# Turning tiles by VectorE blocks and a round trip through DRAM, in one layer of a hybrid decoder

## The chip, the cores and the metric

The kernel runs on one core of a Trainium2 chip. The metric is device time in microseconds. Five engines work side by side, each through its own instructions in order: TensorE (PE in the profile, with PEld for its weight loads), VectorE (DVE), ScalarE (ACT), GpSimd (POOL) and SyncE (SP), which here issues nearly all DMAs.

## The reference

One layer, with 512 prompt tokens (rows) and 8 decode tokens with a past of 1024 keys. All is fp32.

```python
h = einsum('btd,de->bte', x, w_in)             # 1024 -> 256+256+512+16+512 + 4 x 512
qa, ka, va, za, ga, qb, kb, vb, gb = split(h)
# A: gated linear attention, 4 heads, decay from za, state S_t = diag(a_t) S_(t-1) + k_t^T v_t
new_state = exp(b_last)[..., None] * state + einsum('bhsd,bhsv->bhdv', kc * exp(b_last - b), vc)
# B: attention, 8 heads, windows (128,1), (512,4), (2048,16), bias by distance from a table
o_b = prompt_dilated(qb, kb, vb, rel_bias)
mix = concat([o_a * silu(ga), o_b * silu(gb)])
y = einsum('bte,ed->btd', mix, w_out)
x_new = layer_norm(DEEPNORM_ALPHA * x + y, ln_g, ln_b)
```

Outputs are x_new, the new states of A, and the key and value rows of B, for prompt and decode tokens.

## The kernel before

**Products.** An fp32 product is made of three matmuls of parts: the high part of one side by the high part of the other, high by low, and low by high. So every weight tile is loaded (`raw_*`), rounded on ScalarE (`hi_*`), and its rest taken on VectorE (`lo_*`).

**Layouts.** Rows 256 to 511 of the values (va of A, vb of B) and of the output y come out with tokens on partitions, by matmuls of 256 columns (`ps_va_2`, `ps_y`). For rows 0 to 255 the weights stand still in TensorE and 264 columns stream past, 256 prompt rows and the 8 decode tokens. That gives features on partitions (`ps_va_f`, `ps_vb_f`, `ps_yf`), so those tiles have to be turned before they can be used with tokens on partitions. A tile of 128 features (`f`) by 256 tokens is turned by two TensorE transposes of 128x128; two such tiles make a group of 256 columns (`i` or `g`).

- Values: `turn` copies the products to SBUF (`feat`), frees their PSUM bank, and turns into another (`ps_turn`); `va_into` and `vb_into` copy that into `va0` or `v{i}`.
- Decayed keys of A: `gla_state` turns `kd` into `kt` (`ps_kt`), eight transposes and two copies; TensorE then forms the states (`ps_kv`) from `kt` and the values.
- Output: `out_turn` copies to `feat_y`, turns into `ps_yt`, and starts two `out_evac`, which add the result to ALPHA times x in the row tiles `y`, straight from PSUM, with the statistics (`bn_stats`) behind each addition.

**Attention bias.** `bias_table` writes a table `tab` of one row per head to DRAM and copies each row 35 times (`tabr`); `strips` reads, per head and half, a 128-row strip in which each partition is shifted against the one above, with two DMAs for the second half.

**The order of the work.** All is written as generators that yield instructions, marks to wait for (`At`) and buffers to wait for (`Need`, from the slots in `SLOTS`). `add(task, priority)` hands one to `Plan`, which estimates when each waiting instruction could start, by costs in `Op`, and emits the one that starts first; the priority decides between equals. Hence all instructions have line 377 in the profile, and are told apart by their tiles. `dense` with priority 100 is the stream of projections (its sequence is `ORDER`), into which the rest is woven. `LATE` is the planner's allowance for a DMA behind others, and a DMA also waits for the one eight before it (`RING`).

**The end.** `out_first` makes the output of rows 0 to 255, then `out_unit` that of rows 256 to 511 (`ps_y`). The last 256 columns of the last row tile are added up in PSUM on top of x, by `seed` and `last_norm`; the 256 before them go through `early_mean`. The other row tiles are normalized by `norm` as their four statistics are there: a centring with `gamma` and a scaling with `rstd` and `beta`, each a VectorE pass of 128x1024.

Of the kernel before, what the change touches and what calls it, by code (L numbers as in the profile page):

```python
# [20 lines left out]
P = 128  # L21
DM = 1024
KT = DM // P
NP = 512
# [33 lines left out]
T_R = 35  # L58
# [6 lines left out]
SLOTS = dict(  # L65
    g=23,
    w=8, r=3,
    sv=4,
    pt=2, far=5, tp=2, vp=2,
    t2=2, st=3,  # L70
    pr=4,
    t1=5, ob=3,
    m=6)
# [5 lines left out]
LATE = 1000.0  # L79
# [5 lines left out]
ORDER = "qa0 qb0 qb1 qb2 qb3 kb0 kb1 vb0 kb2 kb3 gb0 vb1 gb1 gb2 va0 gb3 va1 ga0 ga1 ga2 ga3".split()  # L85


class Op:
# [3 lines left out]
    def __init__(self, eng, fn, args, kw):  # L92
# [13 lines left out]
        if fn == "dma_start":  # L106
# [4 lines left out]
            rate = 130 if run <= 128 else 175 if x.ap[0][1] <= 64 else 340 if run >= 4096 else 230  # L111
            self.xfer = max(4 * total(x) / rate, 200)
            self.late = 600 * (rate == 175)
# [12 lines left out]
        elif eng.name == "DVE":  # L126
            fast = fn in ("tensor_copy", "tensor_scalar", "memset") and not psum
            ptr = fn in ("tensor_scalar", "scalar_tensor_tensor") and any(size(x) == 1 for x in aps[1:]) and n > 1
            c = ((n / 2 if fast else n) + (155 if fn == "transpose" else 124 if ptr else 66)) / .96
# [7 lines left out]
def run_of(x):  # L137

    n = 1
    for step, c in reversed(x.ap[1:]):  # L140
        if step != n:
            break
        n *= c
    return n

# [236 lines left out]
def trunk(ctx: ExitStack, tc: tile.TileContext, xT, xp, xs, state, ck, cv, w_in, wab, gnorm,  # L382
# [23 lines left out]
    def rsqrt(o, x, scale, eps, between=None):  # L406
# [4 lines left out]
        if between:  # L411
# [3 lines left out]
            add(between, 5)  # L415
# [365 lines left out]
    def dense():  # L781
# [28 lines left out]
        add(gate_decay(pz), 24.7)  # L810
# [66 lines left out]
    def bias_table():  # L877
        yield At("const")
        tab = dram.tile([HB, T_P], F32, name="tab")
# [111 lines left out]
    def gla_state():  # L991
# [120 lines left out]
    def parts(n, own, m, scale):  # L1112

        def evac(ps, u):
# [870 lines left out]
```

## Time and profile before

| | |
|---|---|
| time, 3 runs | 275.93, 277.95, 278.9 us; median 277.95 |
| span of the profiled execution (first to last instruction) | 275.6 us |
| the profiled execution's own time | its span; the nearest timed run, 275.93, is 0.3 above it |
| TensorE busy | 266.9 us (97%) |
| VectorE, ScalarE, GpSimd busy | 214.6, 158.5, 52.8 us |
| DMA | 52.58 MB in 61527 packets, mean 191 GB/s |
| granted TensorE clock | 0.996 |

The span in 40 slices, the busy share in tenths:

```profile
PE   8999999999899999999999999999999999999990
DVE  4845899998989497998396963738999999239984
ACT  4727886475538583877686824535668886224401
DMA  7977939436967898556497979893897660980432
```

A group row gives engine, operation, tile written <- tiles read, shape and count, then the busy time in us and the mean of one in ns, then the idle time ahead of it and who ended it. In a timeline a row is start, duration, engine, line, instruction, and in brackets the wait just before it. A row of the chain is start, length, engine, tile, and how many instructions it joins; its lengths do not overlap.

### The profile page before, as it was taken

Reading aid. Unit: us, or ns where it says so; the run is one execution under the profiler, and the core shown is the slowest. Engines: PE = TensorE matmul, PEld = TensorE weight load, DVE = VectorE, ACT = ScalarE, POOL = GpSimd, SP = SyncE. Lnnn points to the kernel's source line nnn. Section 1 sums busy time; section 2 is a strip of 40 time slices with the busy share of each in tenths; the row PEclk is TensorE's granted clock in tenths of the full one; section 3 lists DMA queues with packets and bytes.
Section 4 is the critical chain, followed back from the end, with each engine's and each line's share of the span. In section 5 each row is a group of like instructions: output and inputs, shape, how many; then the busy total and the mean of one; then the engine's idle time right before and its main releaser. Section 6 shows DMA issues by size and latency. Waiting matters only on the chain.

```text
span 275.6 us, 7460 instructions
## 1 busy us (share of the span) xinstructions
PE 266.9 (97%) x2881; PEld 252.1 (91%) x2881; DVE 214.6 (78%) x578; ACT 158.5 (58%) x478; POOL 52.8 (19%) x71
## 2 busy tenths in 40 slices
PE   8999999999899999999999999999999999999990
PEld 5999999999899989989999999999999999998890
DVE  4845899998989497998396963738999999239984
ACT  4727886475538583877686824535668886224401
POOL 3000000000534260703000633744242000000000
PEclk9999999999999999999999999999999999999998
DMA  7977939436967898556497979893897660980432
GB/s 219 340 181 190 266 91 235 125 104 179 311 188 161 243 291 276 157 115 157 87 258 195 221 202 188 250 279 92 265 246 194 179 223 6 293 239 0 180 129 76
DMA packets 61527, 52.58 MB, mean 191 GB/s; under 512 B 13645, under 2 KB 53715, under 8 KB 61493
## 3 DMA queue, kind: packets, MB, share of 16 engines
q1 hardware_dynamic: 60917, 51.66, 67.2%
q8 instruction: 22, 0.36, 0.5%
q10 hardware_dynamic: 576, 0.46, 0.5%
q14 instruction: 12, 0.10, 0.1%
HBM read 46.02 MB, written 6.42 MB: 190 GB/s over the span
## 4 chain that ended last, share of the span: by engine, by line
PE 94%; DVE 4%; ACT 1%; issue 0%; DVEq 0%
PE ps_ga L377 9%; PE ps_gb L377 9%; PE ps_qb L377 9%; PE ps_yf L377 8%; PE ps_kb L377 8%; PE ps_y L377 7%; PE ps_qa L377 5%; PE ps_ka L377 4%; PE ps_vb_f L377 4%; PE ps_va_f L377 4%; PE ps_vb L377 4%; PE ps_va L377 4%; PE ps_pv L377 3%; PE ps_s L377 3%; PE ps_pt L377 2%; PE ps_oa L377 2%
## 5 line engine op out<-in xcount | busy, mean ns | idle before, releaser
L377 POOL TENSOR_TENSOR past<-past,qbc 128x256 f32<-128x256 f32 x32 | 24.0, 782 | 99.5 <-DMA qbc<-qsd 91.6
L377 POOL TENSOR_TENSOR vv<-vv,pb 128x256 f32<-128x256 f32 x32 | 26.5, 860 | 55.3 <-DMA pb<-psd_s 49.4
L377 ACT ACTIVATE pr<-pr,ms 128x128 f32<-128x128 f32 (+3 forms) x48 | 22.8, 493 | 6.7 <-DVE ms L377 6.5
L377 DVE CUSTOM_DVE_ANT_0 pr<-ps_s,strip 128x128 f32<-128x128 f32 (+3 forms) x32 | 11.8, 410 | 6.9 <-PE ps_s L377 6.0
L377 ACT COPY pt<-ps_pt 128x256 f32<-128x256 f32 (+1 forms) x27 | 9.3, 354 | 11.1 <-PE ps_pt L377 11.1
L377 ACT ACTIVATE sg<-sg 128x264 f32<-128x264 f32 (+1 forms) x32 | 13.4, 420 | 0.5
L377 PE MATMUL ps_ka<-xx,hi_ka 128*128 128x264 f32 (+1 forms) x64 | 12.8, 296 | 0.0
L377 PE MATMUL ps_pt<-cf,pr 128*128 128x128 f32 x56 | 11.0, 274 | 0.0
L377 PEld LDWEIGHTS ps_ka<-xx,hi_ka 128*128 128x128 f32 x64 | 10.4, 201 | 0.0
L377 DVE TENSOR_REDUCE lt<-past 128x8 f32<-128x512 f32 x16 | 10.4, 671 | 0.0
L377 ACT ACTIVATE d<-d 128x512 f32<-128x512 f32 x11 | 6.9, 648 | 5.8 <-DVE d L377 5.8
L377 DVE TENSOR_REDUCE o_pv<-vv 128x4 f32<-128x1024 f32 x8 | 9.7, 1210 | 0.0
L377 ACT COPY feat_y<-ps_yf 128x256 f32<-128x256 f32 x7 | 2.6, 373 | 11.2 <-PE ps_yf L377 11.2
L377 PE MATMUL ps_ka<-xx,lo_ka 128*128 128x264 f32 (+1 forms) x32 | 9.0, 293 | 0.0
L377 DVE SCALAR_TENSOR_TENSOR y<-y,ps_yt 128x256 f32<-128x256 f32 x8 | 3.0, 418 | 6.9 <-PE ps_yt L377 6.9
L377 DVE SCALAR_TENSOR_TENSOR s<-v,ka_s,s 128x128 f32<-128x128 f32 x16 | 5.1, 343 | 3.2 <-DMA v<-vad 1.9
L377 PE MATMUL ps_qa<-xx,hi_ka 128*128 128x264 f32 (+1 forms) x32 | 7.4, 310 | 0.0
L377 PEld LDWEIGHTS ps_pt<-cf,pr 128*128 128x128 f32 x56 | 6.9, 140 | 0.3 <-issue 0.2
L377 PE MATMUL ps_kb<-xx,hi_kb__744 128*128 128x264 f32 (+1 forms) x32 | 6.2, 293 | 0.9 <-DVE ms L377 0.9
L377 PE MATMUL ps_pv<-pt,v 128*64 128x128 f32 (+1 forms) x80 | 6.9, 318 | 0.0
L377 PE MATMUL ps_gb<-xx,hi_gb__1903 128*128 128x264 f32 (+1 forms) x32 | 6.8, 295 | 0.0
L377 ACT CAST xx<-x_raw 128x520 fp32r<-128x520 f32 (+2 forms) x10 | 5.3, 539 | 2.6 <-DMA x_raw<-in_xT_dram 2.3
(570 smaller groups left out, 1065.8 us busy)
## 6 DMA issues: line engine op xcount, KB each, us to landing
past<-in_ck_dram SPq DMA_DIRECT2D x8, 512.0 KB
vv<-in_cv_dram SPq DMA_DIRECT2D x8, 512.0 KB
pb<-psd_s SPq DMA_DIRECT2D x16, 256.0 KB
s<-in_state_dram SPq DMA_DIRECT2D x4, 512.0 KB
strip<-tabr SPq DMA_DIRECT2D x16, 128.0 KB
qbc<-qsd SPq DMA_DIRECT2D x8, 256.0 KB
y<-in_xp_dram SPq DMA_DIRECT2D x4, 512.0 KB
x_raw<-in_xT_dram SPq DMA_DIRECT2D x6, 260.0 KB
```

The costliest lines, as they stand in the source:

```text
L377: getattr(eng.eng, op.fn)(*op.args, **op.kw)
```

## The change

Three kinds of tiles are no longer turned by TensorE. For values and output, VectorE's `transpose` turns each 32x32 block of the PSUM bank into SBUF (`vaw`, `vbw`, `yw`; the bank is free after that). When both tiles of a group are there, `spill` issues four DMAs, one for each 32 partitions, which write the blocks, in runs of 32 elements (128 bytes), to their places in a DRAM scratch (`vsc`, `ysc`). One more DMA reads token rows back, into the value tiles or, for the output, into `yx`, from which `out_evac` adds. The decayed keys go the same way from SBUF (`kx`, `ksc`, then `kt`).

The bias strips come from a table of ready rows, `tabx`, written in DRAM by two DMAs from two smaller tables; a strip is then one DMA. The planner's DMA cost, `LATE`, the cost of a transpose, some slots, many priorities and the place of gb0 in `ORDER` change. `residual` for rows 256 to 511 waits for seven decode columns of the output (`yts`), no longer for `y0_done`; `residual_sample` waits for the state of A.

Three places of the order. First SP at the end of the run, before: `gamma`, `beta` and `y` are the loads of the LayerNorm, `s` and `v` belong to the decode states.

```order
L377 DMA raw_wo__3762<-in_w_out_dram 128x2x512
L377 DMA out_dram<-s_3388 128x8x128
L377 DMA s_3921<-in_state_dram 128x8x128
L377 DMA gamma<-in_ln_g_dram 128x1024
L377 DMA beta<-in_ln_b_dram 128x1024
L377 DMA v_3930<-vad 64x8x128 x2
L377 DMA y_4091<-in_xp_dram 128x1024
L377 DMA y_4093<-in_xp_dram 128x1024
L377 DMA out_dram<-y_3712 128x1024
```

After; the four groups of the output are ysc_95 to ysc_98, and yx are their rows read back:

```order
L377 DMA yx_3933<-ysc_95 128x2x256
L377 DMA yx_3966<-ysc_96 128x2x256
L377 DMA ysc_97<-yw_3950 64x8x32 x3
L377 DMA gamma<-in_ln_g_dram 128x1024
L377 DMA beta<-in_ln_b_dram 128x1024
L377 DMA y_4033<-in_xp_dram 128x1024
L377 DMA y_4035<-in_xp_dram 128x1024
L377 DMA ysc_97<-yw_3950 64x8x32
L377 DMA ysc_98<-yw_4018 64x8x32 x4
L377 DMA yx_4057<-ysc_97 128x2x256
L377 DMA yx_4083<-ysc_98 128x2x256
```

The loads of `gamma`, `beta` and `y` now stand among the scatters of the third group; the scatters of the fourth and the last two reads stand behind them in the same queue.

Second, VectorE's last rows ahead of the chain that ends the kernel. Before, where y_4093 is the last row tile, y_4091 the one ahead of it, and the operands ps_y the products of TensorE:

```order
L377 TENSOR_TENSOR newton<-newton,sums_s 64x1
L377 TENSOR_SCALAR sums_s<-rstd_s 64x1
L377 SCALAR_TENSOR_TENSOR y_4093<-y_4093,ps_y_4170 128x512
L377 TENSOR_REDUCE tail_108<-y_4093 128x1
L377 BN_STATS stats_4094<-y_4093 128x6 x2
L377 TENSOR_SCALAR tail_108<-tail_108 128x1
L377 SCALAR_TENSOR_TENSOR rstd_s<-newton,sums_s 64x1
L377 SCALAR_TENSOR_TENSOR w_s<-w_s,rstd_s 64x128
L377 TENSOR_TENSOR w_s<-w_s 64x128
L377 SCALAR_TENSOR_TENSOR y_4093<-y_4093,ps_y_4238 128x256
L377 BN_STATS stats_4094<-y_4093 128x6
L377 BN_AGGR mv_4271<-stats_4094 128x2
```

After, y_4035 is the last row tile, y_4033 the one ahead of it, y_3726 the second of rows 0 to 255:

```order
L377 SCALAR_TENSOR_TENSOR y_3726<-y_3726,mv_4148,gamma 128x1024
L377 TENSOR_SCALAR newton<-mv_4196 128x1
L377 TENSOR_TENSOR w_s<-w_s 64x128
L377 SCALAR_TENSOR_TENSOR y_3726<-y_3726,rstd_4149,beta 128x1024
L377 SCALAR_TENSOR_TENSOR y_4035<-y_4035,ps_y_4157 128x512
L377 TENSOR_REDUCE tail_117<-y_4035 128x1
L377 BN_STATS stats_4036<-y_4035 128x6 x2
L377 TENSOR_SCALAR tail_117<-tail_117 128x1
L377 SCALAR_TENSOR_TENSOR y_4033<-y_4033,mv_4196,gamma 128x1024
L377 SCALAR_TENSOR_TENSOR y_4035<-y_4035,ps_y_4219 128x256
L377 SCALAR_TENSOR_TENSOR y_4033<-y_4033,rstd_4197,beta 128x1024
L377 BN_STATS stats_4036<-y_4035 128x6
```

The normalizing passes of y_3726 and the centring of y_4033 now stand close ahead of the last row tile's additions, and the scaling of y_4033 stands between the last of these and its statistics. The rows read back (yx) are used 17 rows and more ahead of the first row shown.

Third, SP around the second tile of va, which the GLA state waits for, before (`vad` is a decode scratch, `pb` and `vv` are of the decode attention):

```order
L377 DMA raw_wo__2994<-in_w_out_dram 128x2x512
L377 DMA vv_3008<-in_cv_dram 128x1024
L377 DMA pb_3047<-psd_s 64x4x256 x2
L377 DMA vad<-vat_rows 4x8x128
L377 DMA vv_3113<-in_cv_dram 128x1024
L377 DMA raw_wo__3177<-in_w_out_dram 128x2x512
L377 DMA pb_3181<-psd_s 64x4x256 x2
```

After; vsc_va_102 is that tile's scratch, va_2609 the value tile, s_3113 a half of the decode state.

```order
L377 DMA pb_2966<-psd_s 64x4x256 x2
L377 DMA raw_wo__3019<-in_w_out_dram 128x2x512
L377 DMA vsc_va_102<-vaw_3036 64x8x32 x4
L377 DMA vad<-vat_rows 4x8x128
L377 DMA s_3113<-in_state_dram 128x8x128
L377 DMA va_2609<-vsc_va_102 128x2x256
L377 DMA v_3120<-vad 64x8x128 x2
```

The four scatters and the read are new, and a load of state stands between them.

The core of the diff; most of the priorities, the slots and the planner's costs are left out. No line of context is shown:

```diff
@@ -58 +58,3 @@
-T_R = 35
+T_M = T_P - P
+T_R = T_M + 4
+T_S = 320
@@ -79 +73 @@
-LATE = 1000.0
+LATE = 600.0
@@ -85 +79 @@
-ORDER = "qa0 qb0 qb1 qb2 qb3 kb0 kb1 vb0 kb2 kb3 gb0 vb1 gb1 gb2 va0 gb3 va1 ga0 ga1 ga2 ga3".split()
+ORDER = "qa0 qb0 qb1 qb2 qb3 kb0 kb1 gb0 vb0 kb2 kb3 vb1 gb1 gb2 va0 gb3 va1 ga0 ga1 ga2 ga3".split()
@@ -415 +415 @@
-            add(between, 5)
+            add(between, 21)
@@ -464 +464 @@
-    tabr = dram.tile([HB, T_R, T_P], F32, name="tabr")
+    tabx = dram.tile([HB, P, T_S], F32, name="tabx")
@@ -467,0 +468,3 @@
+    ysc = [dram.tile([GW, GW], F32, name=f"ysc{g}") for g in range(4)]
+    vsc = {n: dram.tile([GW, GW], F32, name=f"vsc_{n}") for n in ("vb0", "vb1", "va0", "va1")}
+    ksc = dram.tile([2 * NP, P], F32, name="ksc")
@@ -719,9 +722,10 @@
-    def turn(ps):
-        f = yield Need("t1", "feat", [P, GW])
-        yield copy(f, ps[:, :GW])
-        free(ps)
-        o = yield bank("t", "ps_turn")
-        for t in range(2):
-            yield T.transpose(o[:, t * P:t * P + P], f[:, t * P:t * P + P], ident)
-        return o, f
+    def spill(blocks, to):
+        for a in range(4):
+            if to.shape[1] == GW:
+                yield D.dma_start(bass.AP(tensor=to.tensor, offset=to.offset + a * 32, ap=[[GW, 32], [P, 2], [32 * GW, 8], [1, 32]]),
+                                  blocks[a * 32:a * 32 + 32].rearrange("p (f b j) -> p f b j", f=2, j=32))
+                continue
+            yield D.dma_start(to[:, a * 32:a * 32 + 32].rearrange("(b i) j -> i b j", i=32),
+                              blocks[a * 32:a * 32 + 32].rearrange("p (b j) -> p b j", j=32))
@@ -879 +883,2 @@
-        tab = dram.tile([HB, T_P], F32, name="tab")
+        tab = dram.tile([HB, 4 * (T_R - 1)], F32, name="tab")
+        tabf = dram.tile([HB, 4, P], F32, name="tabf")
@@ -893 +898,3 @@
-        yield D.dma_start(tab, tsb)
+        yield D.dma_start(bass.AP(tensor=tab.tensor, offset=tab.offset, ap=[[4 * (T_R - 1), HB], [T_R, 4], [1, T_M]]),
+                          tsb[:, None, :T_M].to_broadcast([HB, 4, T_M]))
+        yield D.dma_start(tabf, tsb[:, None, T_M:].to_broadcast([HB, 4, P]))
@@ -895 +902,3 @@
-        yield D.dma_start(tabr, tab[:, None, :].to_broadcast([HB, T_R, T_P]))
+        for src, first, row, step, c, n in ((tab, T_N - P - 1, T_R - 1, -4, T_S - 256, 256), (tabf, 31, P, -1, 0, T_S - 256)):
+            yield D.dma_start(bass.AP(tensor=tabx.tensor, offset=tabx.offset + c, ap=[[32 * T_S, 4 * HB], [T_S, 32], [1, n]]),
+                              bass.AP(tensor=src.tensor, offset=src.offset + first, ap=[[row, 4 * HB], [step, 32], [1, n]]))
@@ -1006,0 +1016,7 @@
+        kx = yield Need("g", "kx", [P, 2, NP])
+        for m in range(2):
+            yield V.transpose(kx[:, m], kd[:, m])
+        free(kd)
+        yield from spill(kx.rearrange("p m t -> p (m t)"), ksc)
+        free(kx)
+        yield At("va_done", TT)
@@ -1008,7 +1024 @@
-        for m in range(2):
-            ps = yield bank("t", "ps_kt")
-            for c in range(TT):
-                yield T.transpose(ps[:, c * P:c * P + P], kd[:, m, c * P:c * P + P], ident)
-            yield copy(kt[:, m].rearrange("p c t -> p (c t)"), ps)
-            free(ps)
-        free(kd)
+        yield D.dma_start(kt.rearrange("p m c d -> p (m c) d"), ksc.rearrange("(k p) d -> p k d", p=P))
@@ -1136 +1146 @@
-                add(keys_out(ps, m, u), 9.7)
+                add(keys_out(ps, m, u), 35.8)
@@ -1173,0 +1184,34 @@
+    def into_rows(n, i, own, to):
+        def evac_f(ps, f):
+            yield copy(own[:, 2 * i + f, :], ps[:, GW:TW[0]])
+            mark(own_mark[n])
+            if f == 0:
+                yield from make(f"{n}w{i}", Need("g", f"{n}w{i}", [P, 2, GW]))
+            else:
+                yield At(f"{n}w{i}")
+            w = B[f"{n}w{i}"]
+            yield V.transpose(w[:, f], ps[:, :GW])
+            free(ps)
+            if f:
+                yield from spill(w.rearrange("p f t -> p (f t)"), vsc[f"{n}{i}"])
+                free(w)
+                yield D.dma_start(to()[:, :2, :], vsc[f"{n}{i}"].rearrange("(t p) c -> p t c", p=P))
+                for _ in range(2):
+                    mark(done_mark(n, i))
+        def evac(ps, t):
+            if n == "vb":
+                yield copy(to()[:, t, :], ps)
+            else:
+                yield copy(B["va1"][:, t - 2, i * GW:i * GW + GW], ps)
+            free(ps)
+            mark(done_mark(n, i))
+        return evac_f, evac
+    own_mark = dict(va="vat", vb="vnt")
+    def done_mark(n, i):
+        return f"vb{i}" if n == "vb" else "va_done"
@@ -1175,15 +1219 @@
-        def evac_f(ps, f):
-            c = slice(i * GW + f * P, i * GW + f * P + P)
-            yield copy(vat[:, 2 * i + f, :], ps[:, GW:TW[0]])
-            mark("vat")
-            ps, f_t = yield from turn(ps)
-            free(f_t)
-            yield copy(B["va0"][:, :, c], ps[:, :GW].rearrange("p (t c) -> p t c", t=2))
-            mark("va_done")
-            free(ps)
-        def evac(ps, t):
-            yield copy(B["va1"][:, t - 2, i * GW:i * GW + GW], ps)
-            free(ps)
-            mark("va_done")
-        return evac_f, evac
+        return into_rows("va", i, vat, lambda: B["va0"][:, :, i * GW:i * GW + GW])
@@ -1192,14 +1222 @@
-        def evac_f(ps, f):
-            yield copy(vnt[:, 2 * i + f, :], ps[:, GW:TW[0]])
-            mark("vnt")
-            ps, raw = yield from turn(ps)
-            free(raw)
-            yield copy(B[f"v{i}"][:, :2, f * P:f * P + P], ps[:, :GW].rearrange("p (t c) -> p t c", t=2))
-            free(ps)
-            mark(f"vb{i}")
-        def evac(ps, t):
-            yield copy(B[f"v{i}"][:, t, :], ps)
-            free(ps)
-            mark(f"vb{i}")
-        return evac_f, evac
+        return into_rows("vb", i, vnt, lambda: B[f"v{i}"])
@@ -1234,4 +1251 @@
-                row = tabr[h]
-                yield D.dma_start(strip[:, 64 * pi:], bass.AP(tensor=row.tensor, offset=row.offset + T_N - P - 1, ap=[[T_P - 1, 4], [T_P - 4, 32], [1, 256]]))
-                if pi:
-                    yield D.dma_start(strip[:, :64], bass.AP(tensor=row.tensor, offset=row.offset + T_P - P + 31, ap=[[0, 4], [T_P - 1, 32], [1, 64]]))
+                yield D.dma_start(strip, tabx[h][:, T_S - 256 - 64 * pi:])
@@ -1647 +1661 @@
-            yield At("y0_done", 4)
+            yield At("yts", 7)
@@ -1737 +1751 @@
-            add(out_evac(t, c // GW, ps[:, :w]), 2)
+            add(out_evac(t, c // GW, ps[:, :w]), 10.4)
@@ -1748 +1762 @@
-            add(out_turn(g, f, p), 2)
+            add(out_turn(g, f, p), 43.7)
@@ -1761,2 +1775,5 @@
-        feat = yield Need("t1", "feat_y", [P, GW])
-        yield copy(feat, ps[:, :GW])
+        if f == 0:
+            yield from make(f"yw{g}", Need("g", f"yw{g}", [P, 2, GW]))
+        else:
+            yield At(f"yw{g}")
+        yield V.transpose(B[f"yw{g}"][:, f], ps[:, :GW])
@@ -1766,7 +1782,0 @@
-        if f == 0:
-            yield from make(f"yt{g}", bank("t", f"ps_yt{g}"))
-        else:
-            yield At(f"yt{g}")
-        for t in range(2):
-            yield T.transpose(B[f"yt{g}"][:, t * GW + f * P:t * GW + f * P + P], feat[:, t * P:t * P + P], ident)
-        free(feat)
@@ -1775 +1785,6 @@
-            plan.share(B[f"yt{g}"], 2)
+            yw = B[f"yw{g}"]
+            yield from spill(yw.rearrange("p f t -> p (f t)"), ysc[g])
+            free(yw)
+            yx = yield Need("g", f"yx{g}", [P, 2, GW])
+            yield D.dma_start(yx, ysc[g].rearrange("(t p) c -> p t c", p=P))
+            plan.share(yx, 2)
@@ -1793,0 +1809 @@
+        yield At("oa_done3")
```

More of the change, by code (lines that the diff above doesn't have):

```diff
@@ L63 @@
 ROWS = 66
[L65 to L73, printed above, removed]
+SLOTS = dict(g=23, w=8, r=3, sv=4, pt=2, far=6, tp=2, vp=2, t2=2, st=2, pr=4, t1=5, ob=3, m=6)
 BANKS = dict(d=3, s=3, t=2)
@@ L109, in __init__ @@
             run = 4 * min(run_of(x) for x in aps)
-            rate = 130 if run <= 128 else 175 if x.ap[0][1] <= 64 else 340 if run >= 4096 else 230
-            self.xfer = max(4 * total(x) / rate, 200)
-            self.late = 600 * (rate == 175)
+            run = min(run, 4096)
+            k = max(j for j in range(1, 17) if all(outer(x) % j == 0 for x in aps))
+            self.xfer = 4 * total(x) / run * max(13, 8.4 + .0368 * run) / k
+            self.late = 0
         elif eng.name == "PE":
@@ L128, in __init__ @@
             ptr = fn in ("tensor_scalar", "scalar_tensor_tensor") and any(size(x) == 1 for x in aps[1:]) and n > 1
-            c = ((n / 2 if fast else n) + (155 if fn == "transpose" else 124 if ptr else 66)) / .96
+            c = ((n / 2 if fast else n) + (92 if fn == "transpose" else 124 if ptr else 66)) / .96
         elif eng.name == "ACT":
@@ L144, in run_of, with outer @@
     return n
+def outer(x):
+    return next((c for _, c in x.ap if c != 1), 1)
 def size(x):
@@ L809, in dense @@
         free(zw, *xraw)
-        add(gate_decay(pz), 24.7)
+        add(gate_decay(pz), 14.6)
         yield from make("ka", Need("g", "ka", [P, 2, NP]), 3)
@@ L1271, in scores @@
             for q in qt:
-                add(softmax(2 * m + v, q, ps[v, q], pr[v, q], cols[q]), 31 + m // 2 / 5 + pi / 10 + m % 2 / 50)
+                add(softmax(2 * m + v, q, ps[v, q], pr[v, q], cols[q]), 34.7 + m // 2 / 5 + pi / 10 + m % 2 / 50)
     def softmax(h, q, ps_all, pr_all, cols):
@@ L1441, in sample_values @@
                                   bass.AP(tensor=row.tensor, offset=row.offset + h2 * 256, ap=[[0, 64], [512, 4], [1, 256]]))
-            add(sample_value(bi, vv, pb), 10.8)
+            add(sample_value(bi, vv, pb), 50.4)
         mark("sv_free")
@@ L1765, in out_turn @@
         free(ps)
[L1766 to L1772 removed]
         mark(f"yt_in{g}")
         if plan.marks[f"yt_in{g}"] == 2:
[L1775 removed]
+            yw = B[f"yw{g}"]
[4 more added lines that the diff above has]
+            plan.share(yx, 2)
             for t in range(2):
[L1777 removed]
+                add(out_evac(t, g, yx[:, t]), 14.6)
     def out_evac(t, g, ps):
@@ L1845, in trunk @@
     warm_ps = plan.alloc(bank("t", "warm_ps"))
-    add(clear(), 0)
+    add(clear(), 8.9)
     add(first_loads(), 0)
-    add(first_splits(), 1)
+    add(first_splits(), 17.6)
     add(fills(), 14.7)
@@ L1865, in trunk @@
     add(mix_sample_a(), 20.7)
-    add(mix_sample_b(), 12.3)
+    add(mix_sample_b(), 9)
     add(ln_rows(), 19.3)
@@ L1880, in trunk @@
         for j in range(2):
-            add(mix_a(pi, j), 16.3)
+            add(mix_a(pi, j), 22.2)
         for m in range(4):
```

1 line of the change is left out of this document (removed).

## The prediction

> **What bounds the kernel now.** I read the busy times first, then the chain of work that ended last, then what is left of idle time on its engine.
>
> ```profile
> span 275.6 us, 7460 instructions
> PE 266.9 (97%) x2881; PEld 252.1 (91%) x2881; DVE 214.6 (78%) x578; ACT 158.5 (58%) x478; POOL 52.8 (19%) x71
> PE 94%; DVE 4%; ACT 1%; issue 0%; DVEq 0%
> core 0: 275.6 us, clock 0.996
> ```
>
> TensorE is busy for 97% of the span and carries 94% of the chain, at a granted clock of 0.996. So a matmul taken away shortens the kernel by the time it holds TensorE alone, unless a wait takes its place. One such wait exists already, in TensorE's timeline, and VectorE's timeline just ahead of it shows its cause:
>
> ```profile
> 73.33 0.28 PE L377 MATMUL ps_kb<-xx,lo_kb__745 128*128 128x264 f32 x1
> 74.57 0.50 PE L377 MATMUL ps_kb<-xx,hi_kb__744 128*128 128x256 f32 x2 [0.95 <-DVE ms L377]
> ...
> 68.61 1.23 DVE L377 TENSOR_TENSOR lo_kb__1214<-raw_kb__871,hi_kb__1213 128x1024 fp32r<-128x1024 f32 x1 [0.95 <-ACT hi_kb__1213 L377]
> ```
>
> TensorE loses 0.95 us there, because VectorE, which works in order, first waits for a weight half and then spends 1.23 us on its low part, ahead of the scores that TensorE needs. The last part of the chain is the end of the run; its VectorE rows come below.
>
> **The turns on TensorE.** The groups of matmuls say how many transposes there are; their 270 to 280 ns overlap with their neighbours, so I take the price from the chain, where each row is the time the chain itself moved on.
>
> ```profile
> L377 PE MATMUL ps_turn<-cf,feat 128*128 128x128 f32 x16 | 3.2, 279 | 0.0
> L377 PE MATMUL ps_yt<-cf,feat_y 128*128 128x128 f32 x16 | 3.0, 271 | 0.0
> L377 PE MATMUL ps_kt<-cf,kd 128*128 128x128 f32 x8 | 1.2, 272 | 0.0
> ...
> 84.41 0.22 PE ps_turn L377 x2
> ...
> 89.95 0.44 PE ps_kt L377 x4
> ...
> 231.73 0.22 PE ps_yt L377 x2
> ```
>
> 0.22 us for two is 0.11 each. 16 + 16 + 8 = 40 of them go, and no other matmul: 40 x 0.11 = **4.4 us less**. The copies on ScalarE and VectorE that surrounded them go too, off the chain.
>
> [...] What the trace shows of that very scheme (blocks from VectorE, DMAs of 128-byte runs) is the storing of the keys:
>
> ```profile
> L377 SPq DMA_DIRECT2D out_dram<-kw x16: 338/507/2096, 77.9 to 119.0; - x16
> L377 DVE STREAM_TRANSPOSE kw<-ps_kb x8: 431/439/468, 67.2 to 111.5; 128x256 f32<-128x256 f32 x8
> ...
> 77.92 6.95 SPq L377 DMA_DIRECT2D out_dram<-kw  x5
> ```
>
> A 128x256 block turn takes VectorE 0.44 us, straight from PSUM; an issue of such a DMA holds SP for 0.51 us in the median, and 6.95 / 5 = 1.39 us in the worst group. Sixteen turns of 0.44 us are 7.0 us more on VectorE, at 78% now, less its share of the copies that go: no bound by the sum, only by its order (below).
>
> **The old stall.** In the new order the 1.23-us low part is gone from that place, and two of half its size (0.69 us each) stand there instead, whose input may be ready. Gain between 0 and 0.95; I take **0.7 us less**, nearer the upper end since only half of the piece stands ahead of the scores at a time.
>
> **The round trips.** A turned tile now takes two transposes, four DMAs that scatter blocks into DRAM, and one that reads rows back. The same write-then-read of DRAM, of the sample scores, stands in the timelines of SP and GpSimd:
>
> ```profile
> 143.69 0.49 SPq L377 DMA_DIRECT2D psd_s<-p_s  x1
> ...
> 147.43 1.33 SPq L377 DMA_DIRECT2D pb<-psd_s  x2
> ...
> 153.20 3.46 POOL L377 TENSOR_TENSOR vv<-vv,pb 128x256 f32<-128x256 f32 x4 [26.91 <-DMA pb<-psd_s]
> ...
> SPq L1981 <- DMA out_dram<-y: 2.1, 1, 2.1
> ```
>
> From the issue of the write to that of the read it is 147.43 - 143.69 = 3.7 us; each read issue holds 1.33 / 2 = 0.7; the data is used 153.20 - 148.76 = 4.4 us later. With 0.44 for the last transpose and three more issues ahead (3 x 0.51 = 1.5), a trip takes 0.44 + 1.5 + 3.7 + 0.7 + 4.4 = **10.8 us**. A short landing, 2.1 us at the end of the run, makes it 8.5; the worst pace of issues (3 x 0.88 more) makes it 13.4.
>
> Who waits? The decayed keys and the first three value tiles are needed far later than that. The tightest is the second tile of va: 85 matmuls stand on TensorE between its last product and the first update of the GLA state that reads it. From
>
> ```profile
> 39.27 9.86 PE ps_qb L377 x82
> ```
>
> one is 0.12 us, so the cover is 10.2 us against 8.5 to 13.4: a wait of 0 to 3.2 us. I take **0.5 more**, from 10.8. SP issues in order, and a load of sample state stands ahead of that read:
>
> ```profile
> s<-in_state_dram SPq DMA_DIRECT2D x4, 512.0 KB
> ```
>
> It is why I do not take zero.
>
> The strips come in 16 DMAs rather than 24, from a table that is written early; TensorE shows no wait on a strip before, and their cover is the whole query and key projection: nothing.
>
> **The end.** Before, turned tiles of y go from TensorE straight into VectorE's additions. The rows I need are the end of the last turned group in the chain, and VectorE's timeline from there:
>
> ```profile
> 244.89 0.97 PE ps_yf L377 x8
> 245.86 2.09 PE ps_y L377 x9
> ...
> 248.21 0.75 DVE L377 SCALAR_TENSOR_TENSOR y<-y,ps_yt 128x256 f32<-128x256 f32 x2 [1.13 <-PE ps_yt L377]
> 248.88 0.75 DVE L377 BATCH_NORM_STATS2 stats<-y 128x6 f32<-128x256 f32 x2
> 249.54 0.25 DVE L377 BATCH_NORM_AGGREGATE mv<-stats 128x2 f32<-128x24 f32 x1
> ...
> 256.30 0.14 DVE L377 COPY sums_s<-ps_ms 64x1 f32<-64x1 f32 x1
> ...
> 261.45 1.29 DVE L377 SCALAR_TENSOR_TENSOR y<-y,rstd,beta 128x1024 f32<-128x1024 f32 x1
> ...
> 263.28 0.69 DVE L377 SCALAR_TENSOR_TENSOR y<-y,ps_y 128x512 f32<-128x512 f32 x1
> ...
> 264.88 0.14 DVE L377 TENSOR_SCALAR tail<-tail 128x1 f32<-128x1 f32 x1
> ...
> 266.28 0.42 DVE L377 SCALAR_TENSOR_TENSOR y<-y,ps_y 128x256 f32<-128x256 f32 x1 [0.51 <-PE ps_y L377]
> 266.73 0.43 DVE L377 BATCH_NORM_STATS2 stats<-y 128x6 f32<-128x256 f32 x1
> ```
>
> Call T the end of the last ps_yf, 245.86. Then the last rows' closing addition starts at T + 20.4 and its statistics at T + 20.9. After the change, the last quarter of rows 0 to 255 comes back from DRAM at T + 10.8. Behind it, in VectorE's order: four operations on it (248.21 to 249.54, 1.3 us); aggregates, two centrings, two scalings, an addition and its statistics (the same kinds as 249.54 to 256.30, 6.8 us); addition, reduction and statistics for the last rows (263.28 to 264.88, 1.6 us); the centring of the third row tile (1.3 us, as the row at 261.45); and some 0.4 us of small ones. That is 11.4 us, so the closing addition starts at T + 22.2, not T + 20.4. Then comes the scaling of the third row tile, 1.2 us alone, which before was over by 262.7, between that addition and its statistics: these start at T + 22.2 + 0.4 + 1.2 = T + 23.8, **2.9 us more**. With the trip at 8.5 us only that inserted scaling counts: T + 20.4 + 0.4 + 1.2 = T + 22.0, 1.1 more. At 13.4 us it is 5.5 more.
>
> The loads of gamma, beta and two x tiles, 2 MB, stand in SP's queue among the last scatters. Before, they ran well ahead of T, with full DMA engines (the last three columns are clock, DMA share and GB/s):
>
> ```profile
> 234.50:241.40 6.90, 6.90 (x59) 6.90 (x59) 1.77 (x6) 1.62 (x7) 0.00 (x0) 1.00 1.02 295
> 241.40:248.30 6.90, 6.90 (x50) 6.46 (x49) 2.22 (x7) 1.47 (x6) 0.00 (x0) 1.00 0.82 225
> ```
>
> At 225 to 295 GB/s they take 7 to 9 us. They are issued when three of the four scatters of the third group are out; that group's last product ends 48 matmuls, 5.8 us, ahead of T, so with 0.44 + 1.5 they start at T - 3.9 and most of them is through when the last read is issued at T + 5.7 (10.8 less 0.7 and 4.4); what is left is why I take the long landing and not the short one.
>
> **Sum.** -4.4 - 0.7 + 0.5 + 2.9 = -1.7 us: a span of 273.9. The fastest timed run (275.93) lies 0.3 above the profiled span, the median (277.95) 2.35; so 273.9 + 2.35 = **276.2 us**, 0.6% less.
>
> **Rival A: the covers hold, and the gain is kept.** Trips of 8.5 us: no wait at the GLA update, and 1.1 at the end: -4.4 - 0.7 + 1.1 = -4.0, so 274.0; with no slip at all 272.9. For it: the short landing is measured, and the pb reads that give 4.4 us are scattered broadcasts. Against it: SP was behind loads at both places. It needs the two waits together under 2.3 us to be faster by 1% (2.8 us, about what a measurement here can tell from no change).
>
> **Rival B: slower, by the pace of the block DMAs.** Each scatter issues as in the worst key group, 1.39 us rather than 0.51, since packets of 128 bytes crowd the queue. Every trip grows by 3 x 0.88 = 2.6 us: 3.1 at the GLA update, 5.5 at the end: -5.1 + 3.1 + 5.5 = +3.5, so 281.5. It is slower by 1% from about 1.26 us an issue (-5.1 + 3.4 + 6x = 2.8, x = 0.75 above 0.51). For it: the group of five at 77.92. Against it: the median of 16. [...]
>
> **Rival C: VectorE blocked in order.** The block turns free PSUM banks, and in the new order stand behind the reductions of past keys that wait for GpSimd; ScalarE can no longer help. A bank held for as long as the old stall's wait (0.95 us), at three of the eight pairs of turns by my estimate, eats 2.9 us: -1.7 + 2.9 = +1.2, so 279.2, within 1%. TensorE's row of waits would name it.
>
> **How the numbers follow.** The forecast has 0.42, of which 0.08 (trips between 8.5 and 10) end more than 1% faster; A 0.33, C 0.08, B 0.17. Faster is thus 0.33 + 0.08 = 0.41, within 1% 0.34 + 0.08 = 0.42, slower 0.17. The range goes from 273.0, short of A's best, to 279.8, past C's 279.2 and half-way to B.
>
> **What would show it.** No ps_turn, ps_yt or ps_kt on TensorE; the stall before ps_kb under 0.3 us; ps_kv waiting about 0.5 us for the read of va; in the last 30 us the yx reads used about 11 us after the last ps_yf, and VectorE working without a gap from there to the last statistics, 23 to 24 us after it (A: 22 or less; B: over 26). A wait of TensorE in the attention for a PSUM bank or the low part of a weight would be C. The forecast is wrong if the trip is not near 10.8 us, since both waits hang on it.

## The result, and the profile after

The changed kernel takes 295.13 us in the median (292.33 to 295.99), against 277.17 for the kernel before: a ratio of 1.063, with a 95% interval of 1.056 to 1.070. The forecast was 276.2, its range 273.0 to 279.8. The kernel is 18 us slower where 1.7 us of gain were expected.

The page and the clock of the changed kernel, the rows that answer to those of before:

```profile
PE 268.6 (91%) x2841; PEld 251.5 (85%) x2841; DVE 221.7 (75%) x610; ACT 145.7 (50%) x438; POOL 52.6 (18%) x71
q1 hardware_dynamic: 86181, 57.43, 73.1%
PE 28%; DVE 28%; DMA 27%; SPq 5%; ACT 5%; issue 4%; POOL 1%; DVEq 0%; ACTq 0%
core 0: 294.2 us, clock 0.962
```

The 40 transposes are gone (2841 matmuls, not 2881), but the chain of work is no longer TensorE's: its share fell from 94% to 28%, and VectorE and DMAs hold as much. The DMA queue carries 86181 packets, where it carried 60917. What TensorE waits for, from the view of waits (total, times, longest):

```profile
PE ps_kv L377 <- DMA va<-vsc_va: 3.5, 1, 3.5
PE ps_va L377 <- DVE vaw L377: 2.6, 1, 2.6
PE ps_dg L377 <- DVE dg L377: 1.6, 1, 1.6
PE ps_pv L377 <- DMA v<-vsc_vb: 1.6, 1, 1.6
```

Before, TensorE waited 0.9 us for one thing, besides the start of the kernel (1.2 us in both). With some smaller ones it is now 13 us, and of the old stall nothing is left. Two of the four large waits are for rows that come back from DRAM, one is for a VectorE that was itself held, and one, at 38 us, has nothing to do with a turn.

The end, from the timelines of TensorE (first row, its last ps_yf) and VectorE:

```profile
258.84 0.28 PE L377 MATMUL ps_yf<-mla,hi_wo__3834 128*128 128x264 f32 x1
...
271.81 0.76 DVE L377 SCALAR_TENSOR_TENSOR y<-y,yx 128x256 f32<-128x256 f32 x2 [0.68 <-DMA yx<-ysc]
...
283.44 0.41 DVE L377 SCALAR_TENSOR_TENSOR y<-y,ps_y 128x256 f32<-128x256 f32 x1
283.77 1.27 DVE L377 SCALAR_TENSOR_TENSOR y<-y,rstd,beta 128x1024 f32<-128x1024 f32 x1
284.97 0.41 DVE L377 BATCH_NORM_STATS2 stats<-y 128x6 f32<-128x256 f32 x1
```

The point called T in the prediction, the end of the last ps_yf, is 259.1 now (258.84 and 0.28), 245.9 before: 13.3 us later. From T to the end of the span it is 35.1 us, and was 29.7. So 13.3 us were lost ahead of T and 5.3 behind it.

### The profile page after: what moved, and what is told of

Its sections match the earlier page's. It is cut to its first block, busy times and chain, and to the rows that moved or that the text cites. A ratio compares the mean times of both kernels' runs of the same rounds, so it can differ in the third digit from the quotient of the medians.

```text
span 294.2 us, 7431 instructions
## 1 busy us (share of the span) xinstructions
PE 268.6 (91%) x2841; PEld 251.5 (85%) x2841; DVE 221.7 (75%) x610; ACT 145.7 (50%) x438; POOL 52.6 (18%) x71
## 3 DMA queue, kind: packets, MB, share of 16 engines
q1 hardware_dynamic: 86181, 57.43, 73.1%
## 4 chain that ended last, share of the span: by engine, by line
PE 28%; DVE 28%; DMA 27%; SPq 5%; ACT 5%; issue 4%; POOL 1%; DVEq 0%; ACTq 0%
DMA strip<-tabx 7%; PE ps_qb L377 6%; SPq L377 5%; PE ps_yf L377 5%; DVE y L377 4%; DMA raw_qb__453<-in_w_in_dram 3%; DMA v<-vsc_vb 3%; PE ps_pv L377 3%; PE ps_va L377 2%; DVE pr L377 2%; DMA v<-vad 2%; PE ps_ga L377 2%; PE ps_vb_f L377 2%; DMA va<-vsc_va 2%; DVE gb L377 2%
## 5 line engine op out<-in xcount | busy, mean ns | idle before, releaser
L377 POOL TENSOR_TENSOR vv<-vv,pb 128x256 f32<-128x256 f32 x32 | 25.9, 838 | 55.6 <-DMA pb<-psd_s 46.1
L377 PE MATMUL ps_pt<-cf,pr 128*128 128x128 f32 x56 | 12.0, 299 | 0.6 <-DVE pt L377 0.4
L377 PE MATMUL ps_ka<-xx,hi_ka 128*128 128x264 f32 (+1 forms) x64 | 12.3, 288 | 0.0
L377 ACT ACTIVATE d<-d 128x512 f32<-128x512 f32 x11 | 6.9, 644 | 10.8 <-DVE d L377 10.8
L377 ACT COPY pt<-ps_pt 128x256 f32<-128x256 f32 (+1 forms) x23 | 8.1, 351 | 6.6 <-PE ps_pt L377 6.5
L377 ACT CAST mhb<-gb 128x256 fp32r<-128x256 f32 x8 | 3.3, 407 | 14.3 <-DVE gb L377 13.8
L377 PEld LDWEIGHTS ps_ka<-xx,hi_ka 128*128 128x128 f32 x64 | 10.2, 196 | 0.0
L377 PEld LDWEIGHTS ps_pv<-pt,v 128*64 128x64 f32 x80 | 5.3, 144 | 3.2 <-DMA v<-vsc_vb 1.8
L377 DVE STREAM_TRANSPOSE yw<-ps_yf 128x256 f32<-128x256 f32 x8 | 3.6, 445 | 5.1 <-PE ps_yf L377 5.1
L377 DVE SCALAR_TENSOR_TENSOR y<-y,yx 128x256 f32<-128x256 f32 x8 | 3.0, 417 | 5.8 <-DMA yx<-ysc 5.8
L377 PE MATMUL ps_va<-hi_va__2213,xx 128*128 128x256 f32 x16 | 4.7, 362 | 2.6 <-DVE vaw L377 2.6
```

Of the source, the lines that this page charges most:

```text
L377: getattr(eng.eng, op.fn)(*op.args, **op.kw)
```

## The experiments

**One part of the change at a time.** First, the new priorities, slots and planner costs without any turn; then all the parts with the old priorities; then the values alone and the output alone.

```diff
# tuning: LATE, SLOTS, ORDER, costs in Op, all priorities, the two At(...); turns and strips as before
# parts: spill, into_rows, kx/ksc, yw/yx, tabx; LATE, SLOTS, ORDER, costs, priorities as before
+        yield At("oa_done3")          # in residual_sample, in parts and in values
# values: into_rows for va and vb only
# output: the new out_turn only
```

> The new priorities, slots, planner costs and waits alone; every tile is still turned by TensorE, and the strips come from the old table. Theory 1 (the loss of 18 us is TensorE waiting for what now comes through DRAM, and the half clock after each such wait): without round trips nothing is late, so within 3 us of before, 274 to 280. Theory 2 (the new order of the work is what delays VectorE and the loads): this alone is slower by 8 us or more, 285 or above.

> All three turns through VectorE and DRAM and the table of ready strips, with the old priorities, slots and planner costs (the decode rows' residual still waits for the state, without which the plan finds no slot). Theory 1: slower than before by 8 us or more, 285 or above, with waits of TensorE at the products of values (ps_pv, ps_kv) of 2 us and more. Theory 2: 40 transposes at 0.11 us gone and little given back, 272 to 277.

> Only the values (va, vb) go through VectorE and DRAM; decayed keys, output and strips as before, old priorities. 16 transposes gone, 1.8 us. Theory 1: the waits at ps_pv and ps_kv, 1.7 and 3.7 us in the changed kernel, appear here with a half clock behind them, so 3 to 9 us slower than before. Theory 2: 1 to 2 us faster.

> Only the output rows 0 to 255 go through VectorE and DRAM; all else as before, old priorities. 16 transposes gone, 1.8 us. The end after the last matmul was 4.5 us longer in the changed kernel. Theory 1: that comes back here whole, so 1 to 4 us slower than before and a gap of 3 us or more more from the last matmul to the end. Theory 2: the end is as before and the kernel 1 to 2 us faster.

Measured: tuning 286.25 us (ratio 1.036, 1.033 to 1.040), parts 309.57 (1.120, 1.117 to 1.123), values 298.99 (1.081, 1.077 to 1.084), output 280.56 (1.016, 1.011 to 1.021). Both theories hold a part of it. `output` fits theory 1: 3.9 us, and 11.2 us from the start of the last matmul to the end, 6.8 before. The new priorities, slots and costs lose 9.6 us with nothing else, so they are no free companion; yet with all the parts they are 14 us better than the old ones. But `values` loses 22 us where theory 1 allowed 9, and its waits do not stand where theory 1 wanted them (those of `parts` do not either):

```profile
PE ps_oat L377 <- DVE oa L377: 9.9, 4, 4.7
PE ps_yf L377 <- ACT mhb L377: 6.8, 1, 6.8
```

These are stages behind the values, in the order that the planner made anew. Since any edit moves the whole order, such a run does not tell a part's own price. The next runs therefore hold the order: the planner reckons with the old instruction, and another is emitted in its place.

**The changed kernel, its order held.** Without scatters; with scatters that no read waits for; with scatters of long runs; with the reads in GpSimd's queue.

```diff
# no_scatter: the planned scatters are not emitted, and, as in no_wait, the reads take rows of x
-  yield D.dma_start(yx, ysc[g].rearrange("(t p) c -> p t c", p=P))
+  yield instead(D.dma_start(yx, ysc[g]...), (nc.sync, (yx, xp[:256, :GW].rearrange("(t p) c -> p t c", p=P))))
# long_runs: a scatter of 32 partitions goes to 32 rows of 2 KB (keys: 4 KB)
+  (nc.sync, (to.rearrange("(p two) c -> p (two c)", two=2)[a * 32:a * 32 + 32], part))
# reads_pool
+  yield instead(D.dma_start(*trip), (nc.gpsimd, trip))
```

> The changed kernel with every instruction in the same order on every engine, but the scatters into DRAM (36 DMAs) left out, and the reads that follow them taking rows of x instead, which lie ready; so turned values, decayed keys and output rows 0 to 255 are wrong, and no round trip is left, only its block turns and its reads. Theory T (the trips themselves are the loss: 128-byte packets that fill the DMA engines, and the wait from write to read): at least 8 us faster than the changed kernel's 295, so 287 or less. Theory Q (the reads and the strips are late because they stand behind bulk loads in SP's one queue): at most 4 us faster, since that queue stays.

> As before in order, with the scatters, but the reads take rows of x, so they wait for no scatter (turned values, decayed keys and output rows 0 to 255 are wrong). Theory T with the wait from write to read as its main part: 4 us or more faster than 295. Theory Q, or T with the traffic as its main part: within 3 us of it.

> The changed kernel in its own order, with all its scatters, reads and waits, but each scatter writes the same 64 or 128 KB in runs of 2 KB or 4 KB per partition instead of 128 bytes (blocks land in the wrong places, so turned values, decayed keys and output rows 0 to 255 are wrong). Leaving the scatters out gained 12.6 us, of which not waiting for them accounts for 3.9. If the rest is the price of 128-byte packets, most of 8.7 us is gained here: 289 or less. If it is the number of DMAs and the time SP takes to issue them, within 2 us of 295.

> The changed kernel in its own order, but the nine reads back are issued by GpSimd, in a queue of their own, not behind SP's loads. Theory Q: the wait at the first ps_pv (1.75 us) and at ps_kv (3.7 us) shrink by half or more, and with the clock behind them 3 to 7 us are gained, 288 to 292. Theory T: no gain beyond 2 us.

Measured: no_scatter 282.51 (1.019, 1.013 to 1.026), no_wait 291.23 (1.049, 1.042 to 1.055), long_runs 285.96 (1.030, 1.026 to 1.033), reads_pool 300.40 (1.082, 1.074 to 1.089). So the scatters cost 12.6 us of the 18, and the wait for their landing 3.9 of them (it fell between the two bounds that were set). Runs of 2 or 4 KB with the same number of DMAs, the same bytes and reads that wait for the same scatters give back 9.2 us. The 9.2 and the 3.9 overlap, for with long runs the waits for rows shrink too. From the waits of long_runs:

```profile
PE ps_kv L386 <- DMA va<-vsc_va: 0.3, 1, 0.3
PE ps_pv L386 <- DMA v<-vsc_vb: 0.2, 1, 0.2
```

Theory Q, that the reads were late because of bulk loads ahead of them, falls: in a queue of their own the waits for rows hardly changed (4.0 us at ps_kv, 1.1 at ps_pv). The 5 us that reads_pool loses come with a new wait, of ps_ys for VectorE:

```profile
PE ps_ys L386 <- DVE lt L386: 5.3, 1, 5.3
PE ps_kv L386 <- DMA va<-vsc_va: 4.0, 1, 4.0
```

How long a scatter holds SP, by tile: min, median and max in ns, first of the changed kernel, then of long_runs:

```profile
L377 SPq DMA_DIRECT2D ysc<-yw x16: 570/635/2382, 247.0 to 263.4; - x16
```

```profile
L386 SPq DMA_DIRECT2D ysc<-yw x16: 320/422/1638, 241.5 to 256.1; - x16
```

Whether the 9.2 us are the longer hold of SP or the many packets in the DMA engines, long_runs cannot say, since both shrink in it (per scatter 0.64 to 0.42 us; in the queue 86181 to 66853 packets).

What is left in no_scatter on TensorE:

```profile
PE ps_dg L386 <- DVE dg L386: 2.1, 1, 2.1
PE ps_oa L386 <- ACT oa L386: 1.9, 1, 1.9
PE ps_va L386 <- DVE vaw L386: 1.9, 1, 1.9
```

The waits for rows are gone, those of the order stand. It is still 6 us slower than before, with 4.4 us of transposes less: 10.4 us that the scatters do not explain. That is near to the 9.6 us of `tuning`, but no proof, for the planner made another order there; that the rest is the order stays an inference.

**The clock.** In the changed kernel the granted clock drops with three of the four larger waits, at ps_pv, ps_va and ps_kv (the last three columns are clock, DMA share and GB/s):

```profile
110.00:120.00 10.00, 8.15 (x58) 7.04 (x57) 8.99 (x21) 3.36 (x10) 6.08 (x8) 0.83 0.95 299
160.00:170.00 10.00, 7.39 (x48) 7.13 (x49) 7.89 (x29) 4.11 (x13) 5.43 (x9) 0.83 0.73 191
200.00:210.00 10.00, 6.51 (x58) 5.81 (x57) 8.09 (x29) 4.75 (x16) 0.00 (x0) 0.67 0.86 235
```

```diff
+ N_KV, N_PV = 30, 14     # matmuls of x by x into the bank that ps_kv, ps_pv are about to overwrite
```

> The changed kernel in its own order, with 44 more matmuls whose result is overwritten: 14 ahead of the first ps_pv and 30 ahead of the first ps_kv, to keep TensorE at work while it waits there. If the half clock that follows each wait comes of the idleness, it is gone in both places, and 2.5 to 5 us are gained, though the kernel does more: 290 to 292.5. If the clock falls for another reason, or costs nothing, the time stays within 1 us of 295.

Measured: 295.46 us (1.058, 1.047 to 1.068), single runs from 291.21 to 297.39: no gain clear of that spread. In its profiled execution the clock was 1.00 in all three stretches, the last of them here:

```profile
200.00:210.00 10.00, 9.78 (x125) 8.91 (x125) 8.98 (x34) 7.08 (x22) 0.00 (x0) 1.00 0.63 180
```

That points to the idleness as what the clock answers to. The stretch near 165 us was not filled, but TensorE had no wait there in this execution either (busy for all 10.00 us), and kept its clock. Against it stands the wait at 38 us in the changed kernel, after which the clock stayed at 1.00 (shown at the end). The profiled execution took 291.21 us at a mean clock of 0.988, the others 295.02 to 297.39 at 0.975 to 0.988; so what the half clock costs here stays open.

**The strips, the order held.** The old table and strip loads in the changed kernel, and the new ones in the kernel before; ahead of the second, the strips alone with the planner free.

```diff
# old_strips: in the changed kernel; strips: the new table in the kernel before, planner free
# strips_in_place: the kernel before in its old order
+  yield instead(D.dma_start(strip[:, 64 * pi:], ...), lambda start, ...: nc.sync.dma_start(strip, tabx[h][:, T_S - 256 - 64 * pi:]))
```

> The changed kernel in its own order on TensorE, VectorE, ScalarE and GpSimd, but with the old table (0.86 MB in one copy) and the old strip loads (24) in place of the new (1.3 MB in two, 16). If the larger table, written while the first weights load, is why VectorE and TensorE wait near 38 us (1.8 us), 1.5 to 4 us are gained, 291 to 293.5; if not, within 1 us of 295, or slower by the eight more loads.

> The kernel before, with only the table of ready strips, old priorities. No matmul goes. If strips cost nothing, as the prediction had it, within 1 us of before; if the larger table delays the first loads, 1 to 4 us slower, with a wait of TensorE before 60 us.

> The kernel before in its old order, with the table of ready strips and its 16 loads. If the table itself costs the 12 us that it lost when the planner was free: 285 or more. If the new order was the cause: within 1 us of before, 276 to 278.5.

Measured: old_strips 312.22 (1.121, 1.114 to 1.129), strips 289.60 (1.045, 1.039 to 1.051), strips_in_place 276.01 (0.9964, 0.9940 to 0.9987). The larger table is no burden; by itself, in an order that fits, it gains 0.4%. The old table with its eight more loads loses 17 us in the changed kernel's full queue, far more than was expected: there VectorE waits in order for strips that come late, and TensorE for VectorE. From the views of waits of old_strips:

```profile
DVE pr L386 <- DMA strip<-tabr: 14.8, 4, 5.8
...
PE ps_va L386 <- DVE vaw L386: 6.9, 1, 6.9
```

So the 12 us that `strips` lost with the planner free were the plan's, not the strips'.

**One part in the old order.** The decayed keys, with the planner free and in place; vb in place; and one number of the planner changed, with no work changed at all.

```diff
# keys: kx, ksc and kt in the kernel before, planner free
# keys_in_place: the transposes are planned and not emitted; where their copies stood:
+  nc.vector.transpose(kt[:, m]..., kd[:, m])       # and for m == 1: spill, and the read 6 us later
# vb_in_place: the same for vb, block turns into the value tile
# one_cost
-  (155 if fn == "transpose" else 124 if ptr else 66)
+  (92 if fn == "transpose" else 124 if ptr else 66)
```

> The kernel before, with only the decayed keys through VectorE and DRAM, old priorities. Eight transposes of 0.11 us and two copies gone; the rows are read long after they are written. Theory T and Q alike: 0.9 us less if nothing waits, 274 to 277; a loss of 2 us or more would say that even one early trip of four scatters disturbs the order.

> The kernel before, every instruction in its old order, except that the eight transposes of decayed keys are gone from TensorE, VectorE turns their blocks where a copy stood, four scatters go out there, and the read back is issued 6 us later in the plan's time. If the part itself costs the 10 us that it lost when the planner was free, it loses them here too, 285 or more. If the new order was the cause, the part alone gains its 8 x 0.11 us or shows nothing: 274 to 278.

> The kernel before in its old order, with only vb going through VectorE and DRAM (eight transposes gone); the read back is issued 6 us after the scatters or ahead of its first user. If trips are cheap where the order leaves room: 275 to 279. If SP, which waits at the read for the scatters and holds up the loads behind it, or the attention, which waits for the rows, is the price: 2 to 8 us slower, 279 to 285.

> The kernel before, with one number of the planner changed (a VectorE transpose is taken to cost 92 + n cycles, as in the changed kernel, not 155 + n): no work changes, only the order in which it stands. If the order alone can lose what the parts lost: 2 us or more slower than before, 279 or above. If the plan is robust: within 1 us.

Measured: keys 288.00 (1.039, 1.035 to 1.042), keys_in_place 281.59 (1.018, 1.015 to 1.021), vb_in_place 290.62 (1.049, 1.045 to 1.054), one_cost 278.58 (1.005, 1.003 to 1.008). The order alone, with one number changed, moves the time by half a percent. The parts themselves cost more. vb loses 13.6 us, more than either guess, and pays at its users, in two waits of ps_pv for its rows (first row below). The keys pay 4.6 us though nobody waits for them; the other rows are SP, VectorE and TensorE of keys_in_place:

```profile
PE ps_pv L400 <- DMA v<-vsc_vb: 9.1, 2, 5.1
...
93.94 6.78 SPq L752 DMA_DIRECT2D ksc<-kt  x4
100.81 0.51 SPq L400 DMA_DIRECT2D raw_gb__1584<-in_w_in_dram  x1
...
106.41 2.08 SPq L400 DMA_DIRECT2D strip<-tabr  x2
...
112.79 0.46 DVE L400 CUSTOM_DVE_ANT_0 pr<-ps_s,strip 128x288 f32<-128x288 f32 x1 [6.83 <-DMA strip<-tabr]
...
114.51 0.79 PE L400 MATMUL ps_gb<-xx,hi_gb__1577 128*128 128x256 f32 x2 [3.77 <-DVE ms L400]
```

Four scatters hold SP for 6.8 us, 1.7 each. The loads behind them go out 6 to 7.5 us later than before, where SP had:

```profile
93.35 0.49 SPq L377 DMA_DIRECT2D raw_gb__1587<-in_w_in_dram  x1
...
100.37 2.33 SPq L377 DMA_DIRECT2D strip<-tabr  x3
```

VectorE comes to the strip, waits 6.8 us in order, and TensorE waits 3.8 for the scores.

**The hold of SP, put to the test.** The same trip of the keys, in place, with the strips of above: its scatters from GpSimd's queue, or from SP but 15 us apart.

```diff
# keys_pool
+  nc.gpsimd.dma_start(to[:, a * 32:a * 32 + 32]...)
# keys_spread
+  plan.later.append((start + (a + 1) * DELAY, ...))      # DELAY 15 us, one scatter each
```

> The kernel before in its old order, with the table of ready strips (0.4% faster by itself, 276.0) and the decayed keys through DRAM, but their four scatters issued by GpSimd, so that SP isn't held; the read back stays on SP. If the hold of SP is the price: the loss of 4.6 us is gone, 274.5 to 277. If the packets in the DMA engines are: 279 or more.

> The same, but the four scatters are issued by SP, 15 us apart in the plan's time, and the read back 15 us behind the last. Each may hold SP for 1.7 us, and the loads behind it have that much room: the loss is gone, 274.5 to 277, if the hold of SP is the price. If the packets are: 277 to 281.

Measured: keys_pool 274.96 (0.9923, 0.9898 to 0.9949), keys_spread 275.01 (0.9929, 0.9904 to 0.9954). The loss is gone in both, and both are faster than either kernel. In keys_pool TensorE waits only at the start of the kernel. Its issues and GpSimd's DMA queue (packets, MB, share), then the issues of keys_spread:

```profile
L756 POOL DMA_DIRECT2D ksc<-kt x4: 786/789/950, 91.7 to 94.2; - x4
...
q0 software_dynamic: 192, 0.52, 0.7%
...
L1070 SPq DMA_DIRECT2D ksc<-kt x4: 422/483/582, 104.8 to 149.6; - x4
```

In keys_pool the packets are not the same: GpSimd's queue carries the 0.52 MB in 192 packets, where SP's takes 4096 of 128 bytes (the page of keys_spread counts 18013 packets under 512 B, that of keys_pool 13917). So that run cannot tell the hold of SP from the packets. In keys_spread SP's queue has all 4096 of them, and the loss is gone too. That points to their standing close together, ahead of loads that somebody waits for, and not to their number, as what cost the 4.6 us. A rival is left: both runs have the new strip loads, fewer than the old ones that came late in keys_in_place, and no run has these with the four scatters together on SP.

## Why the prediction was wrong

**The turns on TensorE** were right: 40 transposes went, and nothing else. Eight of them are worth about what was said where nothing is given back: the two versions of the keys measure 1.0 us less than the strips alone, in separate comparisons, against 0.9.

**The old stall** went, as forecast.

**The round trips: "Who waits? The decayed keys and the first three value tiles are needed far later than that."** This is the step that failed. It asked only who waits for the rows, and put no price on what the scatters hold up on the queue that issues them. The row for it was quoted (6.95 us for five key stores), but its 1.39 us was used only for the length of a trip. In the changed kernel the scatters are worth 12.6 us, 8.7 of them without anybody waiting for their landing, where the sum had 3.4 for the trips. And for the first tiles of vb the cover was there as said, but the trip outlasted it. Block turn and scatters, read, and first user, from the timelines of VectorE, SP and TensorE:

```profile
95.10 0.44 DVE L377 STREAM_TRANSPOSE vbw<-ps_vb_f 128x256 f32<-128x256 f32 x1
...
97.57 3.84 SPq L377 DMA_DIRECT2D vsc_vb<-vbw  x4
...
105.29 1.52 SPq L377 DMA_DIRECT2D v<-vsc_vb  x1
...
113.80 2.05 PE L377 MATMUL ps_pv<-pt,v 128*64 128x256 f32 x16 [1.59 <-DMA v<-vsc_vb]
```

The rows were needed 17.1 us after the block turn (113.80 less the wait), well past 10.8, but the trip takes 18.7: SP works through five other loads between the scatters and the read, and the read lands 8.5 us after its issue.

**The GLA state** was the right place and mis-sized: 3.5 us, not 0.5 (the bounds were 0 to 3.2). The trip from the last block turn to the first user took 12.2 us (192.60 to 204.83), 1.4 more than said. VectorE did that block turn only at 192.60, 3.5 us after the product had ended near 189.1, while the cover was 2.1 us longer than counted (12.3 us from 189.1 to where the wait begins, not 10.2):

```profile
190.09 1.18 DVE L377 TENSOR_REDUCE o_pv<-vv 128x4 f32<-128x1024 f32 x1
...
192.60 0.44 DVE L377 STREAM_TRANSPOSE vaw<-ps_va_f 128x256 f32<-128x256 f32 x1
```

The prediction let the turn start when the product ended.

**"The strips ... nothing"** was right of the strips and wrong of their cover. They gain 0.4% in place; but in the changed kernel one lands 8.3 us after its issue, VectorE meets it in order, and TensorE waits for the block turn behind (2.6 us at ps_va). The chain and VectorE there:

```profile
155.99 8.34 DMA strip<-tabx
...
164.47 0.46 DVE L377 CUSTOM_DVE_ANT_0 pr<-ps_s,strip 128x288 f32<-128x288 f32 x1 [1.36 <-DMA strip<-tabx]
...
165.31 0.44 DVE L377 STREAM_TRANSPOSE vaw<-ps_va_f 128x256 f32<-128x256 f32 x1
```

That is rival C's mechanism with another culprit than it named, at one place rather than three.

**The end** was mis-sized within its bounds. The rows came back at T + 12.7, not 10.8, and the last statistics started at T + 25.9, not 23.8, which with 20.9 before is 5.0 us, not 2.9; the bound was 5.5. The closing addition came 11.6 us after the rows, as worked out (11.4), and the scaling of the third row tile stood behind it. SP and the chain show where the trip grew:

```profile
259.06 6.74 SPq L377 DMA_DIRECT2D ysc<-yw  x5
...
268.93 2.85 DMA yx<-ysc
```

The last five scatters, behind the loads of gamma, beta and x, took SP 1.35 us each, near rival B's 1.39, so that the last read went out at T + 9.8 and not at T + 5.7. It landed faster than said, in 2.9 us and not 5.1.

**The order** was not a term of the sum at all. The sum follows single instructions to their new places, but that the new priorities, slots and costs lose 9.6 us by themselves (`tuning`) was in no rival; how much of the 10.4 us that the scatters leave is this order's stays open. Rival B had the pace of the scatters and the sign, but priced it only on the trips: 281.5. The crowding by packets of 128 bytes that it gave as the cause was an assumption; long_runs, which gives back 9.2 us, does not part it from the hold of SP.

## What to carry to other kernels

Price scatters like these, in packets of 128 bytes, twice: once for who waits for their data (3.9 of the 12.6 us here, by no_wait), and once for what stands behind them on the queue that issues them (in keys_in_place four held SP for 6.8 us, and the loads behind went out 6 to 7.5 us later). Ask which load is next there, and who meets that load in order. Where the data has time, put the scatter on an idle queue or spread it (the 4.6 us of keys_in_place were gone in keys_pool and keys_spread, both with the new strip loads), and do it in the order that is already good: with an order that is made anew, a part's own effect of 1 us drowns in the plan's (1.6 us in one_cost, 9.6 in `tuning`, 13 in `strips`).

## What the runs showed of the hardware

The same four scatters of the keys (1024 packets of 128 bytes each) hold SP for 1.7 us each in one place (keys_in_place), and for 0.48 us in the median when 15 us apart (keys_spread). GpSimd issued them in 0.79 each (keys_pool), and there all four went out in 192 packets rather than 4096.

The granted clock dropped to 0.50 after a wait of 1.6 us (ps_pv, over at 113.8 us), and stayed at 1.00 after another of the same length at 38 us (ps_dg, over at 40.25 us). Windows of the changed kernel:

```profile
38.00:40.00 2.00, 0.62 (x6) 0.40 (x4) 2.00 (x9) 1.94 (x8) 0.00 (x0) 1.00 0.57 144
40.00:42.00 2.00, 1.75 (x15) 1.75 (x16) 1.97 (x8) 0.87 (x2) 0.00 (x0) 1.00 0.41 123
...
116.00:118.00 2.00, 2.00 (x10) 2.00 (x10) 1.49 (x4) 0.91 (x3) 1.37 (x2) 0.50 0.98 346
```
